# In-projection as a Strassen product over pairs of token blocks with HGRN beside it, and RWKV as two streams beside the output projection

## The chip, the cores and the metric

The kernel runs on one core of one Trainium2 chip. A time is the device time of one execution in microseconds (us); the kernel before took 2655.96 us, the median of three runs (2654.36 to 2656.32). The engines are TensorE (PE: matmuls, with its weight loads shown apart as PEld), VectorE (DVE), ScalarE (ACT), GpSimd (POOL) and SyncE (SP). In this kernel POOL and SP mostly issue DMAs. Each engine works through its own list of instructions in order; the order of the lists is fixed when the program is built.

## The reference

One decoder layer over 2048 tokens of width 1024, all in float32.

```python
h = RMSNorm(x)
proj = h @ w_in                                  # 1024 x 3840
q, f, i, g | r, k, v, wd, ad, gd = split(proj)   # 4 x 512 HGRN | 3 x 512 + 64 + 64 + 128 RWKV
o_hg = HGRN2(q, f, i, g)       # 4 heads of 128, gated linear recurrence over tokens, chunkwise
rw = rw + (token_shift(rw) - rw) * mu
o_rw = RWKV7(r, k, v, wd, ad, gd)   # 8 heads of 64, S = S diag(w) + (S a) b^T + v k^T, y = S r
x = x + concat(o_hg, o_rw) @ w_out
x = x + ConvFFN(RMSNorm(x))    # up 1024 -> 2 x 2816, causal conv of 3, silu gate, down 2816 -> 1024
out = RMSNorm(x)
```

Both recurrences carry a state from token to token, so the blocks of 512 tokens must be taken in order.

## The kernel before, in words

The tokens are four blocks of 512 (`BLK`). A float32 product is made of three matmuls of a reduced float32 type: each operand is split into a high and a low part (`split`, lines 250 to 256: a cast on ACT, a subtraction on DVE), and `mm3` (lines 268 to 272) multiplies high by high, high by low and low by high.

The first stage is `phase1`. Its generator `dense` works through a list of jobs: for each block, 30 columns of 128 of the in-projection ("P" jobs, 8 steps of `mm3` over the width of 1024 each, accumulated in a PSUM bank `pj`), the transposes of the next block's normalized input, and, two blocks behind, the output projection of a block (`out_block`) and the norm of its result. The weights of the in-projection are split in the first block and stored in DRAM (`Win`); the later blocks load the two parts again.

Beside it run two more generators. `hg_unit` handles one HGRN head of one block, 16 units in all. `rw_super` handles four RWKV heads of one block, 8 of them in all, one after the other. A `rw_super` scales and groups its inputs, forms the chunk matrices `M`, sends their diagonal 32 x 32 pieces through DRAM into another layout (`Ed`, then `E`), inverts them by 31 dependent steps of two small DVE operations each (lines 800 and 802, tiles `etmp` and `Ti`), transposes the result (`TZ`, `TTs`), runs four groups of small matmuls with evictions between them, and then the eight steps along the tokens (lines 903 to 910, tile `XH`), each needing the one before; a group norm and a gate end it (`yo`).

The main loop of `phase1` takes one step of `rw_super`, one of `hg_unit`, and then fills PE with dense matmuls worth `TICK` = 2000 ns. A step is what lies between two `yield`s. A scheduler then settles each engine's order, roughly in this order, by when it thinks that inputs are there. So the dense matmuls stand between all the small ones until the end of the stage.

Behind `phase1` come the output projection of the last block (`wacc`, line 1268), the up projection of the FFN as a Strassen product over pairs of blocks (seven products of half size in place of eight, tiles `ua`, `ub`, `ud`), and the down projection, also Strassen (`da`, `db`). This part is the same in both kernels.

Of the kernel before, what the change touches and what calls it, by code (L numbers as in the profile page):

```python
# [10 lines left out]
U32 = mybir.dt.uint32  # L11
# [56 lines left out]
def tile_layer(ctx, tc, consts, x, norm1_w, w_in, hg_lb_logits, hg_norm_w, rw_shift_mu, rw_w0, rw_w2,  # L68
               rw_a0, rw_a2, rw_g2, rw_k_k, rw_k_a, rw_r_k, rw_ln_w, rw_ln_b, w_out, norm2_w, w_up,
               conv_w, conv_b, w_down, final_norm_w, out, pairs=(0, 1, 2, 3), heads=(0, 1, 2, 3),  # L70
               stages=("1", "2"), dbg=None):
# [9 lines left out]
    xp_ = cx.enter_context(tc.tile_pool(name="xp", bufs=1, reuse_waits="tile"))  # L81

    def row_tile():
        return xp_.tile([P, 4, D], F32, tag="xt", name="xt", bufs=1)

    ident = cp.tile([P, P], F32, name="ident")
    cst = cp.tile([P, C_ID], F32, name="cst")
    dma(ident, consts[:, C_ID:C_ID + P])
    first = row_tile()
    for i in range(4):  # L90
        dma(first[:, i, :], x[0, i * P:(i + 1) * P, :])
    cen = cst[:, C_CEN:C_CEN + P]
    blk1 = cst[:, C_ONE:C_ONE + P]
    s1m = cst[:, C_S1:C_S1 + P]
    dgm = cst[:, C_DG:C_DG + 64]
    dg32 = cst[:, C_D32:C_D32 + 32]
    scanm = cst[:, C_SCAN:C_SCAN + 512]
# [42 lines left out]
    with tc.tile_pool(name="vp", bufs=1, reuse_waits="tile") as vp, tc.tile_pool(name="ps0", bufs=1, space=PSUM, reuse_waits="tile") as pools["ps"]:  # L140
# [12 lines left out]
        for i in range(4):  # L153
            V.tensor_scalar_mul(first[:, i, :], first[:, i, :], rstd(vp, first[:, i, :], "nst", sqb=2))
# [6 lines left out]

    lnx = cp.tile([P, 4], F32, name="lnx")
    for r0 in (0, 64):
        S.copy(lnx[r0:r0 + 64, :], vt[64 - r0:128 - r0, off["lnw"] + 1:off["lnw"] + 8:2])
# [109 lines left out]
    def phase1(c1):  # L274
        hp = c1.enter_context(tc.tile_pool(name="hp", bufs=1, reuse_waits="tile"))
        wp = c1.enter_context(tc.tile_pool(name="wp", bufs=2, reuse_waits="tile"))
        sp = c1.enter_context(tc.tile_pool(name="sp", bufs=1, reuse_waits="tile"))
        rp = c1.enter_context(tc.tile_pool(name="rp", bufs=1, reuse_waits="tile"))
        ps = c1.enter_context(tc.tile_pool(name="ps1", bufs=1, space=PSUM, reuse_waits="tile"))

        w2a2 = hp.tile([P, 512], F32, name="w2a2")
        g2 = hp.tile([P, 512], F32, name="g2")
        lastc = hp.tile([P, 64], F32, name="lastc")
# [7 lines left out]
        for t_ in (TTs, Af):  # L291
            nc.gpsimd.memset(t_, 0.0)
# [13 lines left out]
        def stg(tag, name, bufs):  # L306
            return sp.tile([P, BLK], F32, tag=tag, name=name, bufs=bufs)
# [1315 lines left out]
```

## Time and profile before

| | us |
|---|---|
| median of three runs | 2655.96 |
| the profiled execution, its own time | 2662.58 |
| span of the profiled execution | 2660.8 |
| PE busy in the span | 2560.2 (96%) |
| DVE busy | 1952.9 (73%) |
| ACT busy | 1389.2 (52%) |
| POOL busy | 380.4 (14%) |

Busy time is the union of the instructions' durations on an engine. PE records overlap (the next matmul starts before the one before has ended), so a PE that is shown busy all the time need not be at its peak, and the distance between two starts says more than a duration. Idle time of an engine is put down to the instruction that ended it. The first `wacc` matmul starts at 1325.8 us, which ends `phase1`; the first `ua` matmul starts at 1373.8 us, and the last down-projection step of the up stage ends at about 2275 us.

### The profile page before, as it was taken

To read this page: it belongs to the slowest core of one execution; us is meant where nothing else is said; L and a number is where in the kernel's file an instruction comes from. 1 tells how busy PE (TensorE), PEld (TensorE's weight loads), DVE (VectorE), ACT (ScalarE), POOL (GpSimd) and SP (SyncE) were. 2 spreads that over 40 slices of the span, in tenths; PEclk is the share of its full clock that TensorE was granted. 3 is DMA by queue.
4 is the path that set the end of the run, shared out by engine and by line. 5 is a ranking of instruction groups with operands and counts; after the bars stand their busy time and mean duration, and the time that the engine had idled before them with its cause. 6 is when DMAs were issued, how large, how long until landed. Compare 5 with 4: busy or idle time off the path is not lost. (4 is left out here: it accounts for less than half of the span.)

```text
span 2660.8 us, 51050 instructions
## 1 busy us (share of the span) xinstructions
PE 2560.2 (96%) x19595; PEld 2061.2 (77%) x19595; DVE 1952.9 (73%) x3728; ACT 1389.2 (52%) x2274; POOL 380.4 (14%) x686
## 2 busy tenths in 40 slices
PE   7999999989999999999899999999999999999998
PEld 5777777766777777777678888887888887888887
DVE  4877667576567765767678789987998887766556
ACT  5566453545535555445456754456545544545444
POOL 6433222212222122222100000000000000000000
PEclk9999999999999999999999999999999999999999
DMA  8645443445643456744493468646763553998665
GB/s 303 204 165 170 158 143 120 130 148 203 199 143 126 156 196 199 276 131 136 154 309 113 143 204 266 233 154 225 245 203 131 166 189 127 327 320 286 197 191 186
DMA packets 312714, 510.59 MB, mean 192 GB/s; under 512 B 46879, under 2 KB 143509, under 8 KB 312469
## 3 DMA queue, kind: packets, MB, share of 16 engines
q1 hardware_dynamic: 257937, 328.99, 37.4%
q0 software_dynamic: 54464, 178.32, 20.4%
q8 instruction: 154, 2.52, 0.4%
q14 instruction: 91, 0.75, 0.1%
q10 hardware_dynamic: 68, 0.02, 0.0%
HBM read 372.99 MB, written 134.22 MB: 191 GB/s over the span
## 5 line engine op out<-in xcount | busy, mean ns | idle before, releaser
L270 PE MATMUL pj<-hh,wh 128*128 128x512 f32 x960 | 393.4, 410 | 6.2 <-ACT rkv L122 3.3
L271 PE MATMUL pj<-hl,wh 128*128 128x512 f32 x960 | 377.8, 394 | 1.3 <-issue 1.3
L272 PE MATMUL pj<-hh,wl 128*128 128x512 f32 x960 | 377.5, 393 | 0.0
L270 PE MATMUL ua<-Bh,uwh 128*128 128x512 f32 x704 | 276.4, 393 | 4.4 <-ACT m L122 3.1
L272 PE MATMUL ua<-Bh,uwl 128*128 128x512 f32 x704 | 274.6, 390 | 0.0
L271 PE MATMUL ua<-Bl,uwh 128*128 128x512 f32 x704 | 274.3, 390 | 0.0
L270 PEld LDWEIGHTS pj<-hh,wh 128*128 128x128 f32 x960 | 181.5, 189 | 55.2 <-issue 8.7
L272 PEld LDWEIGHTS pj<-hh,wl 128*128 128x128 f32 x960 | 181.1, 189 | 40.6 <-issue 1.7
L271 PEld LDWEIGHTS pj<-hl,wh 128*128 128x128 f32 x960 | 181.6, 189 | 34.3 <-DVE hl L488 0.5
L254 ACT CAST uwh<-uraw 128x512 fp32r<-128x512 f32 x220 | 134.2, 617 | 128.9 <-PE ua L271 55.7
L255 DVE TENSOR_TENSOR dal<-draw,dah 128x512 fp32r<-128x512 f32 x138 | 95.4, 691 | 113.4 <-ACT dah L254 113.2
L255 DVE TENSOR_TENSOR uwl<-uraw,uwh 128x512 fp32r<-128x512 f32 x220 | 147.6, 688 | 34.9 <-ACT uwh L254 34.8
L254 ACT CAST dah<-draw 128x512 fp32r<-128x512 f32 x138 | 85.7, 621 | 164.9 <-PE da L271 80.6
L270 PEld LDWEIGHTS ua<-Bh,uwh 128*128 128x128 f32 x704 | 132.2, 188 | 34.1 <-ACT m L122 5.7
L272 PEld LDWEIGHTS ua<-Bh,uwl 128*128 128x128 f32 x704 | 132.3, 188 | 28.1 <-DVE uwl L255 0.4
L271 PEld LDWEIGHTS ua<-Bl,uwh 128*128 128x128 f32 x704 | 132.3, 188 | 26.7
L270 PE MATMUL ud<-Bh,uwh 128*128 128x512 f32 x352 | 138.1, 392 | 0.0
L272 PE MATMUL ud<-Bh,uwl 128*128 128x512 f32 x352 | 137.2, 390 | 0.0
L271 PE MATMUL ud<-Bl,uwh 128*128 128x512 f32 x352 | 137.1, 390 | 0.0
L1493 POOL DMA_DIRECT2D gd<-y x2 | 1.1, 540 | 946.8 <-DVE y L1491 946.8
L271 PE MATMUL da<-dbl,dah 128*128 128x512 f32 x332 | 129.5, 390 | 0.2 <-DVE dbl L255 0.2
L272 PE MATMUL da<-dbh,dal 128*128 128x512 f32 x332 | 129.3, 389 | 0.0
(584 smaller groups left out, 6233.9 us busy)
## 6 DMA issues: line engine op xcount, KB each, us to landing
uraw<-in_w_up_dram SPq DMA_DIRECT2D x176, 256.0 KB, 3.1
woraw<-in_w_out_dram POOLq DMA_DIRECT2D x96, 256.0 KB, 3.6
br<-gd SPq DMA_DIRECT2D x88, 256.0 KB, 4.2
draw<-Sg SPq DMA_DIRECT2D x88, 256.0 KB, 3.3
draw<-Tw SPq DMA_DIRECT2D x88, 256.0 KB, 4.0
gd<-y SPq DMA_DIRECT2D x86, 256.0 KB, 2.9
Sg<-br SPq DMA_DIRECT2D x72, 256.0 KB, 2.1
xt<-x1d SPq DMA_DIRECT2D x32, 512.0 KB, 6.7
```

The costliest lines, as they stand in the source:

```text
L254: S.copy(hi, src)
L255: V.tensor_sub(lo, src, hi.bitcast(F32))
L270: TE.matmul(acc, lh, rh, start=first, stop=False, skip_group_check=skip)
L271: TE.matmul(acc, lh, rl, start=False, stop=False, skip_group_check=skip)
L272: TE.matmul(acc, ll, rh, start=False, stop=last, skip_group_check=skip)
L1493: (dma if end is None else nc.gpsimd.dma_start)(gd_[2 * h + b][fb * P:(fb + 1) * P, :], ys[0][:, b * BLK:(b + 1) * BLK])
```

## The change

`phase1` is replaced by two stages, `phase_a` and `phase_b`. What follows them is unchanged.

**`phase_a`** makes the in-projection of two blocks (1024 tokens) at a time as a Strassen product: two columns of 128 and two blocks of 512 form a 2 x 2 product over two halves of the width, with seven products (`a11`, `a12`, `s2`, `s1`, `s3`, `a22`, `s4`) of 4 steps of `mm3` each. There are 15 pairs of columns (`ORDER`) and two passes, 30 x 7 x 4 x 3 = 2520 matmuls of 128 x 512 in place of 30 x 4 x 8 x 3 = 2880. The seven combinations of the input (`Ah`, `Al`) stand in SBUF; in the first pass they are made by `begin`, in the second from DRAM (`rebuild`). In the first pass the weights and their sums are split and stored (`Win`), in the second loaded. The norm of the later two blocks and the split of `w_out` (`Wout`) run aside. Results are finished per column pair (`column_done`) and stored in DRAM. HGRN's 16 units run beside it, and read their inputs back from DRAM; a unit may start when its `g` column is stored. `hk`, `hf`, `hq`, `hv` and `hg` have one buffer each.

**`phase_b`** then runs RWKV as two streams, each with its own buffers: stream 0 has heads 0 to 3, stream 1 heads 4 to 7; stream 1 starts 24 steps (`LEAD`) later, and a lock lets one stream at a time through the eight steps along the tokens. Beside them run the output projection of blocks 0, 1 and 2, with weights loaded as stored parts, and the norms of blocks 0 and 1.

```diff
+    TICKS = (3200.0, 2200.0)
...
+                    for k in range(KD):
+                        tp = bank("mm")
+                        for i in range(4):
+                            TE.transpose(tp[:, i * P:(i + 1) * P], rows_x[4 * b + i][:, k * P:(k + 1) * P], ident)
+                        act(hT[k][b], tp, AF.Copy, scale=vec("n1", k))
+                        if b == 0:
+                            split_to(Bh[k // 4][:, k % 4, :], Bl[k // 4][:, k % 4, :], hT[k][0])
...
+                    def prod(acc, nm, bi, first, n=n, ops=ops):
+                        wh, wl = ops.pop(nm)
+                        for k in range(4):
+                            mm3(acc, (wh[:, k, :], wl[:, k, :]), (Bh[bi][:, k, :], Bl[bi][:, k, :]),
+                                first and k == 0, k == 3, True)
+                            if k < 3:
+                                yield 680
...
+        credit, at = 0.0, 28
+        while any(alive.values()):
+            if alive["h"]:
+                try:
+                    next(hg_)
+                except StopIteration:
+                    alive["h"] = False
+            credit += TICKS[at >= 15 * 28]
+            while alive["d"] and credit > 0:
+                try:
+                    credit -= next(dn_)
+                    at += 1
+                except StopIteration:
+                    alive["d"] = False
+
+    TICK_B = 1200.0
...
+            while lock:
+                yield None
+            lock.append(s_)
...
+        LEAD = 24
+        gens = [stream(0), stream(1)]
+        dn_ = dense()
+        alive, n, credit = [True, True, True], 0, 0.0
+        while any(alive):
+            for s_ in range(2):
+                if alive[s_] and (s_ == 0 or n >= LEAD):
+                    try:
+                        next(gens[s_])
+                    except StopIteration:
+                        alive[s_] = False
+            credit += TICK_B
...
-        def fill(ns):
-            nonlocal credit
-            credit += ns
-            while alive["d"] and credit > 0:
...
-        while any(alive.values()):
-            for key, g in (("r", rw_), ("h", hg_)):
-                if alive[key]:
-                    try:
-                        next(g)
-                    except StopIteration:
-                        alive[key] = False
-            fill(TICK)
```

Three places in the engines' orders matter below. The first is PE's list at the very start. Before, `hg` and `rw` are PSUM banks lent to the transposes of the first block, and `pj` is the in-projection:

```order
L156 MATMUL vps<-ident,rows 128x128
L264 MATMUL hg<-ident,xt 128x128 x2
L264 MATMUL rw<-ident,xt 128x128
L264 MATMUL hg<-ident,xt 128x128 x2
L264 MATMUL rw<-ident,xt 128x128 x3
L264 MATMUL hg<-ident,xt 128x128 x2
L264 MATMUL rw<-ident,xt 128x128 x2
L264 MATMUL hg<-ident,xt 128x128 x2
L264 MATMUL rw<-ident,xt 128x128 x2
L270 MATMUL pj<-hh,wh 128x512 x2
L271 MATMUL pj<-hl,wh 128x512
```

Now, with `mm` the banks of stage A, and `Al_75` to `Ah_78` the tiles that hold the rows of blocks 0 and 1 at first:

```order
L361 MATMUL mm<-ident,Al_77 128x128 x12
L361 MATMUL mm<-ident,Ah_78 128x128 x12
L361 MATMUL mm<-ident,Al_77 128x128 x2
L361 MATMUL mm<-ident,Ah_78 128x128 x2
L361 MATMUL mm<-ident,Al_77 128x128 x2
L361 MATMUL mm<-ident,Ah_78 128x128 x2
L264 MATMUL mm<-Ah_63,uwh 128x512
L265 MATMUL mm<-Al_64,uwh 128x512
L266 MATMUL mm<-Ah_63,uwl 128x512
```

Before, the first dense matmul followed half of one block's transposes; now all 64 transposes of two blocks (the first 32 stand ahead of these rows) come first.

The second place is PE's list at the end of HGRN. Before, the last unit's matmuls (`hg`) stand among dense ones (`pj`) and RWKV's (`rw`):

```order
L272 MATMUL pj<-wh,hl 128x512
L1081 MATMUL rw<-part,group 128x512
L1082 MATMUL rw<-part,group 128x512
L1081 MATMUL rw<-part,group 128x512
L1082 MATMUL rw<-part,group 128x512
L1081 MATMUL hg<-part,ones 128x512
L1082 MATMUL hg<-part,ones 128x512
L270 MATMUL pj<-wh,hh 128x512
L271 MATMUL pj<-wl,hh 128x512
L272 MATMUL pj<-wh,hl 128x512
```

Now a whole unit, from its first transposes (L656) to its norm (L269, L270), and with it the unit ahead of it, stands alone between the last dense matmul of stage A and the first matmul of RWKV (L891, which follows the last L270):

```order
L269 MATMUL hg<-part,ones 128x512
L270 MATMUL hg<-part,ones 128x512
L656 MATMUL hg<-ident,hv 128x128 x4
L695 MATMUL hg<-hq,hk 32x32 x16
L695 MATMUL hg<-hX 32x16 x80
L702 MATMUL hg<-hX 32x32 x8
L749 MATMUL hg<-ident,hk 128x128 x4
L751 MATMUL hg<-hX 64x64 x4
L760 MATMUL hg<-VT,KT 128x128 x4
L770 MATMUL hg<-Af,VT 128x128
L771 MATMUL hg<-hq,SH 128x128
```

After the last dense matmul PE's list has the norm of unit 13 and all of units 14 and 15 (16 units are counted from 0), and then RWKV.

The third place is DVE's list around an inversion. Before, the 62 small operations (`etmp`, `Ti`) have HGRN's between them (`hf`, `hk`, `hq`, `hX`):

```order
L802 TENSOR_TENSOR Ti<-Ti,etmp 128x10x11
L972 TENSOR_TENSOR hf<-hf 128x4x64
L800 TENSOR_TENSOR etmp<-E,Ti 128x108
L1035 TENSOR_TENSOR hk<-hk,Sf 128x512
L802 TENSOR_TENSOR Ti<-Ti,etmp 128x9x12
L1036 TENSOR_TENSOR hq<-hq,hf 128x512
L800 TENSOR_TENSOR etmp<-E,Ti 128x96
L963 TENSOR_TENSOR hX<-hq,hf 128x256
L802 TENSOR_TENSOR Ti<-Ti,etmp 128x8x12
```

Now, where stream 1's first inversion ends (`TTs_9617` is stream 1's) and stream 0's second begins:

```order
L1019 TENSOR_TENSOR Ti<-Ti,etmp 128x16
L1023 STREAM_TRANSPOSE TZ<-Ti 128x512
L1029 STREAM_TRANSPOSE TTs_9617<-TZ 32x16x32 x4
L1008 MEMSET Ti 128x512
L1098 COPY XH<-Xc 128x2x64
L1010 COPY Ti<-cst 128x16 x2
L951 TENSOR_TENSOR M<-rw,cst 128x2x2x128 x4
L1089 TENSOR_TENSOR M<-rw,cst 128x2x4x64
L1092 TENSOR_TENSOR AR<-rw,AR 128x2x4x64
L1017 TENSOR_TENSOR etmp<-E,Ti 128x31
L1019 TENSOR_TENSOR Ti<-Ti,etmp 128x31
```

L1089 and L1092 are stream 1's, and read PE's result of the matmuls that use its new `TTs`; stream 0's inversion (the last two rows) stands behind them. HGRN's operations are gone from this stage.

1164 lines of the change are left out of this document (625 added, 539 removed).

## The prediction

> **What bounds the kernel now.** I read the busy times by stage first, then the distance between the starts of neighbouring instructions, then the groups by line, then single waits. Busy time by stage (columns: stretch, its length, PE, PEld, DVE, ACT and POOL busy with their counts, granted PE clock, DMA share, GB/s):
>
> ```profile
> 0.00:20.00 20.00, 4.55 (x17) 3.04 (x17) 8.13 (x27) 11.99 (x28) 12.78 (x27) 1.00 0.91 305
> 20.00:1326.00 1306.00, 1239.79 (x13778) 976.18 (x13778) 888.12 (x2106) 668.67 (x1105) 351.85 (x631) 0.99 0.52 171
> 1326.00:1374.00 48.00, 45.49 (x196) 35.95 (x196) 34.03 (x57) 23.85 (x42) 1.82 (x3) 1.00 0.92 308
> 1374.00:2275.00 901.00, 892.79 (x3946) 734.46 (x3945) 780.75 (x1177) 500.59 (x762) 0.19 (x1) 1.00 0.57 188
> 2275.00:2661.00 386.00, 377.54 (x1663) 311.57 (x1662) 241.83 (x364) 184.09 (x340) 13.80 (x26) 0.99 0.75 252
> ```
>
> The change replaces the first 1326 us and leaves the other 1335 as they are. The first stage is bound by PE: 95% busy, DVE 68%, ACT 51%. What PE does there, as the same view gives it for the instructions on one bank name (dense `pj`, RWKV `rw`, HGRN `hg`, in this order):
>
> ```profile
> 20.00:1326.00 1306.00, 900.45 (x3616) 654.74 (x3616) 88.03 (x167) 100.13 (x160) 0.99 0.52 171
> 20.00:1326.00 1306.00, 271.35 (x6153) 211.69 (x6152) 121.40 (x196) 159.53 (x244) 0.99 0.52 171
> 20.00:1326.00 1306.00, 136.81 (x4008) 115.28 (x4008) 60.59 (x180) 54.92 (x116) 0.99 0.52 171
> ```
>
> A dense matmul with a few transposes costs 900.45/3616 = 0.249 us beside the small work; in the FFN, which has none, 892.79/3946 = 0.226 us. RWKV costs 271/8 = 34 us of PE a super, HGRN 137/16 = 8.6 us a unit. DVE's share is held by many lines; first and last of RWKV's 31 groups and of HGRN's 16:
>
> ```profile
> L802 DVE TENSOR_TENSOR Ti<-Ti,etmp 128x126 f32<-128x126 f32 (+22 forms) x248 | 63.3, 255 | 4.5
> L685 DVE MEMSET W<- 128x16 f32 x8 | 0.6, 72 | 11.9 <-PE rw L893 11.9
> L972 DVE TENSOR_TENSOR hf<-hf 128x256 f32<-128x256 f32 x112 | 47.3, 422 | 1.2
> L1057 DVE COPY Sc<-SH 128x128 f32<-128x128 f32 x16 | 3.5, 218 | 0.2
> ```
>
> Their sums are 429 us (53.6 a super) and 296 us (18.5 a unit). Durations on DVE overlap a little, as starts in the timeline show (start, duration):
>
> ```profile
> 1219.84 0.24 DVE L802 TENSOR_TENSOR Ti<-Ti,etmp 128x81 f32<-128x81 f32 x1
> 1220.12 0.24 DVE L800 TENSOR_TENSOR etmp<-E,Ti 128x78 f32<-128x78 f32 x1
> ...
> 1254.36 0.67 DVE L255 TENSOR_TENSOR wl<-woraw,wh 128x512 fp32r<-128x512 f32 x1
> 1254.96 0.67 DVE L413 TENSOR_TENSOR xh<-pj,xh 128x512 f32<-128x512 f32 x1
> ```
>
> An independent 128x512 operation takes 0.60 us, 0.87 of its duration of 0.69 (the groups' mean, below); the dependent steps of the inversion take 0.28 each, however idle the engine is.
>
> **Stage A, dense part.** Durations that the next parts use (a subtraction of a split; an eviction and a cast on ACT; four transposes, the next group starting 0.56 us later):
>
> ```profile
> L255 DVE TENSOR_TENSOR wl<-woraw,wh 128x512 fp32r<-128x512 f32 x96 | 65.8, 688 | 32.9 <-ACT wh L254 32.5
> L122 ACT ACTIVATE h<-pj,vt 128x512 f32<-128x512 f32 x16 | 10.3, 684 | 8.2 <-PE pj L264 7.8 <-ACT h L122 0.4
> L254 ACT CAST wh<-wraw 128x512 fp32r<-128x512 f32 x60 | 36.9, 619 | 75.4 <-PE pj L271 36.5 <-DMA wraw<-in_w_in_dram 15.2 <-issue 9.6
> 127.42 0.63 PE L1042 MATMUL hg<-ident,hk 128*128 128x128 f32 x4 [1.59 <-DVE hk L1035]
> 127.98 0.68 PE L1044 MATMUL hg<-hX 128*64 128x64 f32 x8
> ```
>
> The Strassen form removes 2880 - 2520 = 360 matmuls, 82 to 90 us at the two rates. RWKV's stalls are gone from beside it, HGRN's stay, so I take 0.236, between them. DVE stays below PE: in the first pass a pair needs some 22 us of it (seven splits and seven sums at 0.69, 2.6 for finishing columns, 2.6 aside, 0.4 unit of HGRN), or 19 by starts, against 84 x 0.236 + 0.4 x 8.6 + 1 = 24 us of PE. The stores and loads of weights leave POOL's queue for SP's, where a store that waits for a split holds the loads behind it; two operands of lag cover that, and without the cover each product (12 matmuls, 2.8 us) would wait for a landing of some 3 us.
>
> The start is later. Before, PE's first matmul waits for a small load, and in the first 20 us it has 4.55 us of work:
>
> ```profile
> L156 PE MATMUL vps<-ident,rows 128*128 128x128 f32 x1 | 0.4, 448 | 10.7 <-DMA rows<-in_hg_lb_logits_dram 10.7
> ```
>
> Now 64 transposes and 16 evictions on ACT (0.69 each, with eight casts of 0.62 and eight half squares of about 0.6, together 21 us) stand ahead of the first product, so it starts near 40. The first pair needs 16 subtractions and 20 splits more on DVE, 36 x 0.60 = 22 us; at 65 us PE has done 96 matmuls. Bounds: 42 us (96 x 0.226 behind a start at 20) and 85 (nothing beside anything). The rest is 2424 x 0.236 = 572, fourteen units of HGRN 14 x 8.6 = 120, and 128 transposes at 0.14 are 18. The last dense matmul is at 65 + 572 + 120 + 18 = **775 us**.
>
> [...]
>
> **Stage A, HGRN alone.** As the order shows, units 14 and 15 run with no dense matmul beside them. Nothing in the trace shows a unit alone. From below it costs PE's 8.6 us; from above the 54 us that unit 15 took beside dense work, from its first DVE operation at 1257.4 to its last matmul at 1311.1. Its own chain: about 14.5 us of dependent DVE work by starts (of 18.5), some 4 us of ACT (evictions and casts of 0.60, Ln and Exp), 5 us of PE, and the wait for its predecessor's store, since `hk` and `osq` share a buffer:
>
> ```profile
> L945 DVE TENSOR_SCALAR hk<-hf 128x512 f32<-128x512 f32 x16 | 6.8, 423 | 4.1 <-DMA oT<-osq 4.0
> oT<-osq POOLq DMA_DIRECT2D x4, 256.0 KB, 3.0
> 1257.42 0.47 DVE L945 TENSOR_SCALAR hk<-hf 128x512 f32<-128x512 f32 x1 [0.59 <-DMA oT<-osq]
> L1063 PE MATMUL hg<-hq,SH x128: 270/275/580, 134.0 to 1311.1; 128*128 128x128 f32 x128
> ```
>
> That is 27 us; two, and the end of unit 13, make **60 us** (17 to 112). PE idles for most of it; before, dense matmuls filled these gaps.
>
> **Stage B.** PE's work is 271 + 576 x 0.226 + 14 = 415 us, DVE's 429 + 52 (splits of the heads' outputs, residual sums, norms) = 481, or 418 by starts. Eight supers with no overlap set the other bound. One super's chain alone: front (sigmoids, scan, some fourteen 1.0 to 1.2 us operations) 26, `M` 6.5, the trip through DRAM 6.4, inversion 62 x 0.28 = 17.4, transposes 3.9, four groups of matmuls with evictions between them 16.5, eight steps at 0.87 (see below) 7, group norm 14: 97 us, so 776 for eight. The rows for the trip, two of the evictions, a front operation, `M`, a transpose, and two steps:
>
> ```profile
> Ed<-M SPq DMA_DIRECT2D x32, 64.0 KB, 3.3
> E<-Ed SPq DMA_DIRECT2D x16, 256.0 KB, 3.1
> L122 ACT ACTIVATE UV<-rw 64x512 f32<-64x512 f32 x32 | 19.0, 593 | 0.6 <-PE rw L845 0.2
> L122 ACT ACTIVATE ZT<-rw 32x256 f32<-32x256 f32 x32 | 12.0, 375 | 6.0 <-PE rw L819 5.5
> L717 DVE TENSOR_TENSOR ai<-ai 128x1024 f32<-128x1024 f32 x8 | 9.8, 1220 | 0.0
> L733 DVE TENSOR_TENSOR M<-rw,cst 128x512 f32<-128x512 f32 x64 | 40.4, 685 | 11.0 <-PE rw L730 10.9
> L812 DVE STREAM_TRANSPOSE TTs<-TZ 32x512 f32<-32x512 f32 x32 | 22.5, 703 | 0.8
> 1286.17 0.29 DVE L910 TENSOR_TENSOR XH<-rw,WC 128x128 f32<-128x128 f32 x1
> 1287.04 0.29 DVE L910 TENSOR_TENSOR XH<-rw,WC 128x128 f32<-128x128 f32 x1
> ```
>
> DVE's order says how the two streams mesh. It repeats three parts. X: stream 1's front (14 us by starts), two sums and eight steps of stream 0, stream 1's `M`, and the trip through DRAM, before which stream 1 can't invert: 36 us. Y: stream 0's group norm (14), its front and its `M`, and between them stream 1's inversion, of which 8.5 us are left over, and transposes: 49 us. Z: stream 1's groups of matmuls, for whose first result (L1089) DVE waits some 12 us with stream 0's inversion queued behind it, then that inversion with stream 1's steps in it, 21, and transposes: 37 us. A round is 122 us. Stage B is stream 0's first front to transposes (56, its first squares being done ahead), three rounds (366), a last X (36), the last inversion alone (21), groups, steps and norm (42), and 49 dense matmuls that PE's list has behind them (11): **532 us**. It lies nearer to 418 than to 776 because the two fronts and inversions do overlap in the list. The output projection is hidden in it, and of no use to it: it can't fill DVE's waits.
>
> **The sum.** 775 + 60 + 532 + 1335 = 2702 us of span. The profiled run took 2662.58 for a span of 2660.8, so 2704 for this one; it lay 6.6 above the median, so **2697**, 41 us slower than before.
>
> **Rivals.** *The streams fill each other's gaps* (faster). If DVE never waits in the order above, stage B needs its 418, plus stream 0's head start and stream 1's end at half use, some 50: 468. With stage A ending at 763 (at 0.231) and a tail of 50, the span is 2616 and the time **2611**. For it: DVE reaches 781/901 = 87% in the FFN. Against it: there the order runs ahead of need, here 62-step chains, a trip of 6.4 us and the L1089 wait stand in one queue. It turns to faster when a round is below 110 us.
>
> *One queue, two streams* (slower still). If waits of both streams add up in DVE's and PE's lists, since an output-projection matmul placed early waits for heads just stored, a round grows by 25 us to 147; three and a half rounds give 88 more: **2785**. For it, waits of one engine for another's list are long now (24 here, the longest 12.4 us):
>
> ```profile
> ACT rkv L122 <- PE pj L272: 135.6, 24, 12.4
> ```
>
> Against it, the lists were sorted by readiness.
>
> *PE runs cold.* After a PE idle stretch the profile grants half the clock:
>
> ```profile
> 1285.00:1290.00 5.00, 2.77 (x61) 2.01 (x56) 4.49 (x14) 2.78 (x7) 0.54 (x1) 1.00 0.93 305
> 1290.00:1295.00 5.00, 3.85 (x9) 3.08 (x10) 2.17 (x5) 2.97 (x5) 0.00 (x0) 0.51 0.80 273
> ```
>
> Here 2.2 us idle were followed by a clock of 0.51. Such gaps are rare now, 0.99 on the mean; units 14 and 15 and stream 0's head start are made of them, and stage B has 415 us of PE work in 532. If half of stage B runs at half clock, the some 20 us of PE on a super's chain cost 10 more, 10 x 5 (four supers and the head start) plus 10 in the tail: **2757**. [...]
>
> *The change does not do what it says*: HGRN beside the product for fourteen units of sixteen is settled by the list, so this has no time of its own.
>
> **How the numbers follow.** Forecast 0.50 (own range 2660 to 2735, 0.05 of it within 0.2% of before, about what a measurement can tell from no change), streams filling gaps 0.28, one queue 0.12, cold PE 0.10. Faster 0.28, same 0.05, slower 0.67. The range takes in the faster case with its bounds for the start and the tail, and most of the slower ones: 2605 to 2790.
>
> **What would show it.** The last dense matmul of stage A near 775 us; a stretch of some 60 us with only `hg` matmuls; RWKV's last matmul near 1350; DVE about 87 to 90% busy in stage B with waits of about 10 us at L1089 and at the first `etmp` after `E`; a granted clock near 1 in the first 750 us and lower after. A stage B below 490 us, or a stage A that ends before 750, makes the prediction wrong.

## The result, and the profile after

The changed kernel takes 2879.03 us (median of four runs, 2873.91 to 2889.03) against 2656.14 for the kernel before (median of four runs): a ratio of 1.084, 95% interval 1.080 to 1.088, 223 us slower. The sign is the one forecast; the time is far outside the range. Its profiled execution has a span of 2872.1 us, 170 more than the 2702 of the sum.

Busy time by stage of the changed kernel (columns as before: stretch, its length, PE, PEld, DVE, ACT and POOL busy with their counts, granted PE clock, DMA share, GB/s):

```profile
20.00:798.00 778.00, 727.59 (x6089) 578.10 (x6090) 516.42 (x1144) 390.82 (x742) 85.05 (x157) 0.97 0.81 277
798.00:862.00 64.00, 29.77 (x531) 24.06 (x531) 40.47 (x110) 21.12 (x43) 8.56 (x15) 0.63 0.23 75
862.00:1543.00 681.00, 501.98 (x6785) 363.13 (x6784) 448.40 (x1001) 325.20 (x496) 104.44 (x195) 0.85 0.49 161
1543.00:1590.00 47.00, 45.33 (x195) 35.86 (x195) 33.05 (x55) 24.13 (x43) 0.00 (x0) 1.00 0.92 302
1590.00:2491.00 901.00, 895.82 (x3965) 736.22 (x3964) 784.57 (x1183) 504.57 (x767) 1.08 (x2) 1.00 0.58 189
2491.00:2872.00 381.00, 373.49 (x1646) 308.25 (x1644) 237.18 (x358) 180.96 (x334) 12.92 (x24) 1.00 0.75 254
```

The last dense matmul of stage A starts at 798.2 us, HGRN alone lasts until 861.7, the RWKV stage until the first `wacc` matmul at 1542.8, and the rest takes 1329.4. Of the 170 us, stage A has 23, the HGRN tail 3.5, the RWKV stage 149 (681.0 where 532 were forecast), and the rest takes 5.6 less. In the RWKV stage no engine is near full: PE 74%, DVE 66%, ACT 48%, at a clock of 0.85. The same view for the instructions on one bank name (`pj`, `rw`, `xp`, `yp`, in this order) tells what PE did there:

```profile
862.00:1543.00 681.00, 196.92 (x640) 117.85 (x640) 16.45 (x24) 14.21 (x32) 0.85 0.49 161
862.00:1543.00 681.00, 240.52 (x4096) 171.92 (x4094) 90.83 (x120) 149.23 (x232) 0.85 0.49 161
862.00:1543.00 681.00, 56.59 (x1024) 41.41 (x1024) 18.43 (x64) 0.85 0.49 161
862.00:1543.00 681.00, 55.85 (x1024) 44.33 (x1024) 9.54 (x16) 0.85 0.49 161
```

RWKV is the sum of the last three rows, 353 us for eight supers, where the kernel before had 271; a projection matmul or transpose takes 196.92/640 = 0.31 us. Both are larger in a stage with a clock of 0.85. The groups by line of that stage show where engines stood still (behind the bar: busy, mean ns of one; then the idle time ahead of them and what ended it):

```profile
L264 PE MATMUL pj<-wh,oh 128*128 128x512 f32 x192 | 88.1, 471 | 46.9 <-ACT oh L248 17.3 <-DMA wh<-Wo03h 9.3 <-DVE xh L1182 5.7
L249 DVE TENSOR_TENSOR ol<-oraw,oh 128x256 fp32r<-128x256 f32 x48 | 19.9, 421 | 14.5 <-ACT oh L248 14.4
L248 ACT CAST oh<-oraw 128x256 fp32r<-128x256 f32 x48 | 18.6, 402 | 68.7 <-DMA oraw<-oT 54.0 <-PE pj L265 14.6
L1132 DVE TENSOR_TENSOR XH<-xp,WC 128x128 f32<-128x128 f32 x64 | 18.4, 288 | 29.8 <-PE xp L1125 29.1
L1182 DVE TENSOR_TENSOR xh<-pj,xh 128x512 f32<-128x512 f32 x24 | 16.4, 689 | 23.7 <-PE pj L266 23.6
L1089 DVE TENSOR_TENSOR M<-rw,cst 128x512 f32<-128x512 f32 x16 | 11.0, 688 | 34.3 <-PE rw L1086 34.3
```

Four of the six lines belong to the projection (`pj`, `oh`, `ol`, `xh`): PE, ACT and DVE each wait for it, with the streams' instructions queued behind. The round can be read off the timeline of DVE, from one scan of stream 1's front to the next:

```profile
924.81 1.22 DVE L898 TENSOR_TENSOR_SCAN mk<-cst,ai 128x512 f32<-128x512 f32 x1 [0.73 <-ACT ai L120]
...
1063.94 1.23 DVE L898 TENSOR_TENSOR_SCAN mk<-cst,ai 128x512 f32<-128x512 f32 x1 [1.71 <-ACT ai L120]
...
1217.48 1.22 DVE L898 TENSOR_TENSOR_SCAN mk<-cst,ai 128x512 f32<-128x512 f32 x1
...
1380.87 1.22 DVE L898 TENSOR_TENSOR_SCAN mk<-cst,ai 128x512 f32<-128x512 f32 x1 [2.13 <-ACT ai L120]
```

Rounds of 139, 154 and 163 us, where 122 were forecast. The first ends before the projection really begins: 36 of its 576 matmuls have run by then.

### The profile page after: what moved, and what is told of

It is laid out like the page before. It is cut to its first block, busy times and chain, and to the rows that moved or that the text cites. A ratio compares the mean times of both kernels' runs of the same rounds, so it can differ in the third digit from the quotient of the medians.

```text
span 2872.1 us, 51606 instructions
## 1 busy us (share of the span) xinstructions
PE 2580.7 (90%) x19235; PEld 2051.2 (71%) x19235; DVE 2066.9 (72%) x3869; ACT 1460.2 (51%) x2451; POOL 216.1 (8%) x405
## 4 chain that ended last, share of the span: by engine, by line
PE 39%; DMA 6%; DVE 4%; issue 1%; ACT 1%; SPq 1%; POOL 0%; DVEq 0%; ACTq 0%; POOLq 0%
PE ua L264 4%; PE ua L266 4%; PE ua L265 4%; PE da L264 3%; PE da L265 3%; PE da L266 3%; PE ud L265 2%; PE ud L266 2%; PE ud L264 2%; PE db L264 2%; PE db L265 2%; PE db L266 2%; DMA br<-gd 1%; PE ub L265 1%; PE ub L266 1%
## 5 line engine op out<-in xcount | busy, mean ns | idle before, releaser
L264 PE MATMUL mm<-Ah,uwh 128*128 128x512 f32 x840 | 349.6, 416 | 29.4 <-ACT m L120 20.0
L266 PE MATMUL mm<-Ah,uwl 128*128 128x512 f32 x840 | 337.6, 403 | 6.6 <-DMA uwl<-Win54l 4.4
L265 PE MATMUL mm<-Al,uwh 128*128 128x512 f32 x840 | 336.7, 401 | 0.6 <-DVE Al L242 0.6
L248 ACT CAST uwh<-uraw 128x512 fp32r<-128x512 f32 x295 | 180.7, 618 | 195.5 <-PE ua L265 58.7
L249 DVE TENSOR_TENSOR uwl<-uraw,uwh 128x512 fp32r<-128x512 f32 x295 | 198.4, 686 | 53.4 <-ACT uwh L248 52.6
L264 PEld LDWEIGHTS mm<-Ah,uwh 128*128 128x128 f32 x840 | 160.9, 192 | 72.4 <-ACT m L120 25.3
L266 PEld LDWEIGHTS mm<-Ah,uwl 128*128 128x128 f32 x840 | 160.9, 192 | 48.7 <-DMA uwl<-Win54l 4.5
L265 PEld LDWEIGHTS mm<-Al,uwh 128*128 128x128 f32 x840 | 161.2, 192 | 34.9 <-DVE Al L242 1.7
L248 ACT CAST uwh<-s 128x512 fp32r<-128x512 f32 x118 | 72.4, 620 | 133.1 <-PE ua L265 62.6
L264 PE MATMUL pj<-wh,oh 128*128 128x512 f32 x192 | 88.1, 471 | 46.9 <-ACT oh L248 17.3
```

Source lines behind the costliest of these rows:

```text
L248: S.copy(hi, src)
L249: V.tensor_sub(lo, src, hi.bitcast(F32))
L264: TE.matmul(acc, lh, rh, start=first, stop=False, skip_group_check=skip)
L265: TE.matmul(acc, lh, rl, start=False, stop=False, skip_group_check=skip)
L266: TE.matmul(acc, ll, rh, start=False, stop=last, skip_group_check=skip)
```

## The experiments

Except for ticks_low each kernel was timed once, so the lengths of stages are compared. The RWKV stage goes from its first matmul to the first `wacc` matmul. The same code does not repeat exactly: the RWKV stage of the changed kernel took 681.0, 686.8 and 691.6 us in three runs that leave it alone, and the last dense matmul of an untouched stage A came between 793 and 806. Differences under 10 us are not read. The 681.0 from which differences are taken below is the lowest of its three, so a gain against it may be up to 10 us larger, and a loss as much smaller.

| run | last dense matmul | RWKV stage | its last RWKV matmul, from its first | time |
|---|---|---|---|---|
| changed kernel | 798.2 | 681.0 | 658.5 | 2879.03 |
| no_proj | 798.5 | 577.6 | 571.1 | 2772.58 |
| fill | 801.7 | 582.4 | 575.6 | 2779.28 |
| one_stream | 804.2 | 370.7 | 362.5 | 2570.75 |
| one_fill | 799.7 | 364.3 | 356.1 | 2561.89 |
| proj_only | 797.1 | 626.7 | 618.5 | 2824.27 |
| proj_loose | 800.2 | 665.3 | 649.8 | 2860.75 |
| no_proj_late | 794.9 | 583.3 | 576.6 | 2772.09 |
| late_rhs | 800.9 | 682.4 | 647.4 | 2877.42 |
| pool_side | 799.4 | 704.0 | 681.7 | 2902.47 |
| prefetch | 803.7 | 703.0 | 612.8 | 2903.17 |
| tick_b_high | 800.3 | 700.3 | 693.5 | 2896.29 |
| dve_fill | 793.0 | 586.2 | 579.4 | 2783.18 |
| act_fill | 802.7 | 582.4 | 575.6 | 2784.69 |
| all_fill | 799.9 | 588.1 | 581.4 | 2796.77 |
| dve_placed | 805.6 | 604.6 | 594.7 | 2803.06 |
| all_placed | 798.2 | 610.1 | 600.0 | 2803.21 |
| no_hgrn | 681.0 | 686.8 | 663.4 | 2703.84 |
| ticks_low | 864.7 | 691.6 | 668.2 | 2888.16 |

**The streams alone.**

```diff
-        alive, n, credit = [True, True, True], 0, 0.0
+        alive, n, credit = [True, True, False], 0, 0.0
```

> The output projection, the norm and the sums of token blocks 0 to 2 are left out of the RWKV stage (their outputs are set to zero by 56 stores), the two streams stay as they are. In the changed kernel this stage took 681 us, from the first RWKV matmul to the first matmul of the next stage, with 179 us of PE idle and a granted clock of 0.85. Theory 1 (PE runs cold: idle stretches halve its clock, and what PE does on the streams' chains takes longer): there are more idle stretches now, the clock falls below 0.8, and the stage stays near 600. Theory 2 (the projection's matmuls and loads stand in the streams' queues): the stage falls to the 520 that I had forecast, three rounds of about 122. Theory 3 (the round of two streams was sized too small in itself): the stage stays above 630 and a round near 150.

577.6 us: between the theories, 103 less than the changed kernel, and yet 46 more than the 532 forecast for the whole stage. So the two streams were sized too small, and the projection is far from hidden. The row of the stage, and stream 1's scan, its next scan and what stood between the end of stream 0's steps and stream 1's inversion:

```profile
862.00:1440.00 578.00, 347.64 (x6145) 262.62 (x6146) 398.91 (x904) 283.54 (x385) 1.26 (x2) 0.75 0.14 42
```

```profile
1195.23 1.22 DVE L898 TENSOR_TENSOR_SCAN mk<-cst,ai 128x512 f32<-128x512 f32 x1 [1.64 <-ACT ai L120]
...
1228.95 0.23 DVE L1135 COPY Xc<-XH 128x128 f32<-128x128 f32 x1
1235.95 1.23 DVE L242 TENSOR_TENSOR part<-yo,part 128x1024 fp32r<-128x1024 f32 x1 [6.77 <-ACT part L241]
1241.61 1.23 DVE L1145 TENSOR_TENSOR yo<-yo 128x1024 f32<-128x1024 f32 x1 [4.44 <-ACT yo L120]
1242.76 0.18 DVE L1017 TENSOR_TENSOR etmp<-E,Ti 128x31 f32<-128x31 f32 x1
...
1333.61 1.22 DVE L898 TENSOR_TENSOR_SCAN mk<-cst,ai 128x512 f32<-128x512 f32 x1 [1.74 <-ACT ai L120]
```

A round is 138 us here. Part X, from stream 1's scan to its inversion, is 1242.8 - 1195.2 = 47.5 us where 36 were forecast: after stream 0's last step DVE works 2.5 of 13.6 us, since stream 0's norm stands in its list ahead of stream 1's inversion and waits twice for ACT. The trip through DRAM was also longer than forecast: its first store is issued at 1226.3 us and the last packet of its loads ends at 1235.4, 9.1 us for 6.4 (the forecast had one store and one load behind each other; there are four stores and two loads). So of the 11.5 us some 3 are the trip's, and the 7.4 from 1235.4 to 1242.8 are the norm's. Parts Y and Z take 91 together, against 86.

**Free matmuls beside the streams.** Matmuls of zeros, written at the projection's places of the program:

```diff
+            acc = bank("pj")
+            for q in range(24):
+                TE.matmul(acc, group, zt, start=q == 0, stop=q == 23)
+                if q % 3 == 2:
+                    yield 680
```

> As no_proj, but the 576 projection matmuls are replaced by as many matmuls of the same size, into the same two banks and at the same places of the program, whose operands are always there (no loads, splits or evictions). Theory 1: the clock rises to over 0.9 and the stage is shorter than in no_proj, by some 40 us, though PE does 130 us more. Theory 2: if it is the waiting of the projection for its data that hurts, the stage is as in no_proj within 15 us; if it is its mere time on PE, it is as in the changed kernel, near 680. Theory 3: as in no_proj.

```profile
865.00:1448.00 583.00, 471.86 (x6794) 359.64 (x6794) 399.07 (x904) 284.43 (x385) 1.25 (x2) 0.89 0.14 41
```

The program has 648 of them, not 576, and they did not stay at the projection's places: waiting for nothing, they were put between 870 and 1261 us, 375 of them ahead of the time from which the projection runs (1064 us). PE is busy 124 us more, the clock goes from 0.75 to 0.89, and the stage stays where it was. The same holds within one round: stream 1's round from 1064 to 1204 us, full of such matmuls at a clock of 0.95, took 140 us, and that of no_proj from 1060 to 1195 us 136 at 0.79. Neither the matmuls' time on PE nor the half clock bounds the streams, or the two cancel; the next pair tells.

**One stream, bare and with matmuls.**

```diff
-        alive, n, credit = [True, True, True], 0, 0.0
+        alive, n, credit = [True, False, False], 0, 0.0
```

> As no_proj with the second stream left out as well (two of the four heads' pairs are not computed): four supers one behind the other, and nothing beside them. My prediction put one super's chain alone at 97 us: 4 x 97 = 390 from its first matmul to its last. Theory 1: the clock is near 0.6, and a super takes 110 to 115 us, 450 in all. Theory 2 leaves it at 390. Theory 3: the chain itself was sized too small, over 120 us a super at a clock that is not the reason.

> one_stream with 576 matmuls of zeros, free of dependencies, in the gaps of the one stream; some 65 of them fall behind its end. One stream alone took 362.5 us from its first matmul to its last at a clock of 0.68, 92 a super. Theory 1 (the half clock lengthens a chain): the clock rises over 0.9 and a super takes 82 to 85 us. If a super stays at 91 to 93, the half clock costs the chain nothing that matters, or the filler takes back what it gives.

```profile
865.00:1229.00 364.00, 182.19 (x3073) 138.12 (x3073) 204.23 (x450) 138.52 (x188) 4.26 (x8) 0.69 0.13 40
```

```profile
862.00:1220.00 358.00, 294.48 (x3649) 226.50 (x3649) 204.05 (x451) 138.96 (x188) 4.26 (x8) 0.90 0.13 40
```

A super takes 362.5/4 = 91 us at a clock of 0.69 and 356.1/4 = 89 at 0.90: the chain was sized well (97). The matmuls of one_fill all run by 1093 us, none behind the stream's end; so the first two supers are the cleaner pair, 183 us at 0.69 (869 to 1053 us in one_stream) and 180 at 1.00 (866 to 1046 in one_fill). The lower clock costs some 2 us a super, less than the runs repeat, net of what the free matmuls take on PE. Theory 1 falls. One super uses DVE for 204/4 = 51 us; two streams in a round of 138 use it for 100.

**What order can mend.** The block that makes `RHS` and `UV` is written later, so that ACT comes to stream 0's norm first:

```diff
+            def late_rhs():
                 RHS = tile_("KB", [8, 2, P], "RHS")
...
             for j in range(31):
...
+                if j == 7:
+                    RHS, UV = late_rhs()
```

> no_proj (streams alone, 577.6 us for the stage, a round of 137) with the block that makes RHS, UV and the first correction (lines 976 to 1005) written behind the eighth step of its stream's inversion instead of ahead of it. In the trace of no_proj DVE stood still 29.6 us ahead of the norm's split and 25.2 us ahead of the norm's product, since on ACT the evictions of the other stream's RHS and UV stood ahead of the norm's square and cast, and the other stream's inversion stood behind the norm on DVE. If that order is what made the round 14 us longer than the 122 forecast, those two idle sums fall under 20 us together, the round to about 126 and the stage to 535 to 545. Rival: the round is bound elsewhere and the idle moves to other rows; the stage stays above 565.

> The same edit on the whole changed kernel (stage 681 us). By the order of ACT 35 to 45 us less, 640; by the rival 670 or more.

The idle of 55 us ahead of the norm's two operations (no_proj) fell to 28, and came back elsewhere, ahead of the next front's scan and of the norm's sum with `BV`. The groups in no_proj, then those in no_proj_late (whose lines behind the inversion are numbered two higher):

```profile
L898 DVE TENSOR_TENSOR_SCAN mk<-cst,ai 128x512 f32<-128x512 f32 x16 | 19.5, 1220 | 9.5 <-ACT ai L120 9.5
L242 DVE TENSOR_TENSOR part<-yo,part 128x1024 fp32r<-128x1024 f32 x8 | 9.8, 1223 | 29.6 <-ACT part L241 29.6
L1152 DVE TENSOR_TENSOR yo<-yo,BV 128x1024 f32<-128x1024 f32 x8 | 9.7, 1213 | 3.3 <-ACT yo L120 3.3
L1145 DVE TENSOR_TENSOR yo<-yo 128x1024 f32<-128x1024 f32 x8 | 9.7, 1219 | 25.2 <-ACT yo L120 25.2
```

```profile
L898 DVE TENSOR_TENSOR_SCAN mk<-cst,ai 128x512 f32<-128x512 f32 x16 | 19.5, 1221 | 30.2 <-ACT ai L120 30.2
L1147 DVE TENSOR_TENSOR yo<-yo 128x1024 f32<-128x1024 f32 x8 | 9.8, 1225 | 16.8 <-ACT yo L120 16.8
L1154 DVE TENSOR_TENSOR yo<-yo,BV 128x1024 f32<-128x1024 f32 x8 | 9.8, 1225 | 18.8 <-ACT yo L120 18.8
L242 DVE TENSOR_TENSOR part<-yo,part 128x1024 fp32r<-128x1024 f32 x8 | 9.8, 1223 | 11.0 <-ACT part L241 11.0
```

The stage stayed at 583, and at 682 with the projection. The order of ACT makes this wait and not the length of the round: with half of the wait gone, as much idle stands elsewhere in the same round. What sets the round, as I read it, is that a chain of 91 us runs through lists which also hold the other chain's 50 us of DVE work, and finds its own waits filled only in small part: 91 + 50 = 141, near the 136 to 138 measured. That sum fits, but no run proves it.

**The projection taken apart.** First without norm and sums, then with matmuls that do not read what was loaded:

```diff
-                if nb < 2:
-                    yield from norm_block(nb)
...
-                            mm3(accs[q], [t_[:, q * P:(q + 1) * P] for t_ in held[k]], wts, k == 0, k == KD - 1)
+                            mm3(accs[q], (group, group), (zt, zt), k == 0, k == KD - 1)
```

> The norm and the sums of the finished blocks are left out of the RWKV stage, the output projection with its loads stays. no_proj showed 578 us for the stage without all three, the changed kernel 681. Theory 2a (the projection itself holds the streams back: its matmuls stand in PE's list and wait for their loads and splits): the stage stays above 655. Theory 2b (the norm and the sums do, with their DVE and ACT work and their chains of loads and stores on SP's queue): the stage falls to 600 to 620.

> Everything stays beside the streams (loads, splits, evictions, norm, sums), but the projection's 576 matmuls read a fixed tile of zeros in place of the operands just loaded, so that PE never waits for them; ten buffers of splits become eight to make room. Theory 2a: if PE's waiting for the projection's data holds the streams back, the stage falls to under 610. Rival (the extra work on DVE and ACT, 50 and 42 us more busy time, and the loads): it stays above 645.

Each half carries about half of the cost: 49 us for the projection alone, 54 more for norm and sums. Without PE's waits for data the stage is 16 us shorter, of the 103. The run is not quite the changed kernel without these waits: it has eight buffers for ten, and 192 of its matmuls, free to go, ran before 1000 us (28 in the changed kernel). Theory 2a, that PE's waits do most of it, falls.

**Moving the side work, or asking earlier.**

```diff
-                            held.append(split(wp, raw, [P, 256], "o", 10))
+                            S.copy(hi, raw)
+                            nc.gpsimd.tensor_sub(lo, raw, hi.bitcast(F32))
```

> The changed kernel with the DVE work of the projection's side moved to POOL, which is idle in this stage: the subtractions of its splits (48 of 128x256), the scaling of the norm (8 of 128x1024) and the four sums (16 of 128x512), some 39 us of DVE. no_proj is 103 us shorter than the changed kernel, proj_only 54, and proj_loose only 16, so it is not PE that waits. Theory Q (side work stands in DVE's list between the two streams' steps, with its waits): the stage falls by 35 to 60 us, to 620 to 645. Rival (ACT's share and the loads hold the streams): it falls by less than 15.

```diff
+                            while len(raws_) < min(k + 3, KD):
...
+                                dma(raw, oT[nb][k_ * P:(k_ + 1) * P, i2 * 256:i2 * 256 + 256])
...
+                    yield 1500
                     for q in range(2):
                         V.tensor_add(xh[q], accs[q], xh[q])
```

> The changed kernel with the projection's operands asked for earlier: each load of a row block of heads is written two blocks ahead of its split, and 1500 units of time lie between a group's last matmul and its eviction on DVE. In the changed kernel ACT stood still 68.7 us ahead of the casts of these blocks (mostly for their loads) and DVE 23.7 us ahead of the evictions and 14.5 us ahead of the splits. If these waits in the lists of ACT and DVE are what costs, the stage falls to 640 to 650 and the idle ahead of the casts under 30; if it is the mere work, it stays within 10 us of 681.

```diff
-    TICK_B = 1200.0
+    TICK_B = 2400.0
```

> The changed kernel with twice the pace at which the projection is put between the streams' steps (2400 units a step for 1200). Its last matmul now comes 21 us behind the streams' last. If the pace only shifts the cost, the streams end later by what the projection ends earlier, and the stage stays within 10 us of 681; if the projection was merely late, the stage falls to 660.

All three made the stage longer, by 19 to 23 us. With POOL, 37 us of work left DVE's list (19.9 + 5.8 + 11.1), whose busy time fell by only 12 (448 to 436), in part since operations that stayed became slower (shown in the last section), and on POOL the moved ones took longer themselves (a subtraction 894 ns for 421). POOL also issues the loads of the projection's weights, and the moved subtractions now stand between these; PE's idle ahead of its first matmuls for such a load hardly grew (9.3 to 10.2 us). How much of the 23 us each makes was not separated. With prefetch the streams ended 46 us sooner (612.8), with 424 of the stage's 448 us of DVE work done by then, and the projection 89 us behind them: the delay of the streams went and came back as the projection's own end. ACT stood still even longer ahead of the casts. At the double pace the projection was done 40 us ahead of the streams, which took 35 us more: DVE waited 62.9 us for a step's product, for 29.8 before. The group of the casts in prefetch, then that of the steps at the double pace:

```profile
L248 ACT CAST oh<-oraw 128x256 fp32r<-128x256 f32 x48 | 18.4, 402 | 103.4 <-DMA oraw<-oT 91.1 <-PE pj L265 9.4 <-issue 2.9
```

```profile
L1132 DVE TENSOR_TENSOR XH<-xp,WC 128x128 f32<-128x128 f32 x64 | 18.5, 289 | 62.9 <-PE xp L1125 62.4
```

So the pace shifts the cost between the streams and the projection, and saves none of it.

**Work without data.** Additions on DVE and copies on ACT that wait for nothing:

```diff
+                    V.tensor_add(fz[:, 0], fz[:, 1], fz[:, 1])
+                    act(fz[:, 2], fz[:, 3], AF.Copy)
```

> no_proj (streams alone, 577.6 us) with 72 additions of 128x512 on DVE that depend on nothing, spread as the projection is: 50 us of busy time, 43 by starts, as much as the projection, the norm and the sums put on DVE. If DVE's list is the path (it shows 69% busy, but the streams' chains stand in it), the stage grows by 35 to 50, to 613 to 628. If the cost is in waits for data, it grows by less than 15.

> The same with 72 copies of 128x512 on ACT, some 45 us, as much as the projection's casts, squares and evictions. If ACT's list (49% busy) is on the path too, the stage grows by 20 or more; if only DVE's is, by less than 10.

> 72 additions on DVE, 72 copies on ACT and 576 matmuls beside the streams, none of which waits for anything: all of the projection's work without its data. The changed kernel with the data is at 681. If the work is what costs, the stage is at 640 or more; if the data, under 600.

These three grew by 5 to 11 us, but say little: having nothing to wait for, the operations were placed early. The 72 on DVE ran between 805 and 905 us, 42 of them in the idle HGRN tail. The additions and copies were repeated, each held behind the stream's operation that precedes it:

```diff
+                    tc.add_manual_dep(i_.ins, mark["d"].ins.name, NOSYNC, reason="place")
```

> no_proj (577.6 us) with 72 additions of 128x512 on DVE, 43 us by starts, each held in DVE's list at its place among the streams' operations of rounds 2 to 4, with no data to wait for. If DVE's list is the path and mere work counts, the stage is at 610 to 625. If DVE has room for it between the streams (31% idle), it is under 590.

> As dve_placed, and 72 copies on ACT held at their places in the same way, and 576 matmuls that wait for nothing. If work is what costs, the stage is at 640 or more, near the 681 of the changed kernel; if the waits for data are, under 610; between the two, the part above 578 is the work's and the rest the waits'.

```profile
862.00:1472.00 610.00, 470.27 (x6721) 356.20 (x6720) 441.63 (x978) 324.71 (x456) 1.98 (x3) 0.85 0.14 42
```

27 us for DVE's work alone (43 by starts), and 32 with ACT's and PE's added. PE, DVE and ACT are now as busy as in the changed kernel but for 32, 7 and 0 us (first stage view), and the stage is 71 us shorter. So of the projection's 103 us a third is the price of DVE's and ACT's work in lists that have room on paper. The matmuls were not held: 383 of the 576 ran before 1064 us, so their price at the projection's own places is not in the 32.

The other 71 are a remainder, and that they come with the data (waits for loads and for each other) is argued and not shown. The trace says where they stand: against all_placed DVE works 7 us more and is idle 64 us more. Of its idle in the changed kernel 38 us stand right ahead of the projection's splits and evictions (14.5 and 23.7, the rows above) and 8 ahead of the norm and the sums. Some 12 are the longer end (the next stage starts 22.5 us behind the streams' last matmul, 10.1 in all_placed). The projection's traffic did not slow the streams' own trip through DRAM: to 1440 us a store of `Ed` lands in 2.0 us (2.2 in no_proj), a load of `E` in 3.6 (4.0). Which waits make the 71 was not taken apart beyond proj_loose and prefetch.

**Stage A, without HGRN and with HGRN placed denser.**

```diff
-            for n in range(16):
+            for n in range(0):
                 while len(units) <= n:
```

> The 16 units of HGRN are left out of the first stage (their rows of the output are set to zero), the dense product stays. My sum had 0.236 us for a dense matmul beside HGRN and 8.6 us of PE for a unit: by it the last dense matmul comes at 65 + 572 + 18 = 655 us. The changed kernel's trace has 93 us of PE time between dense matmuls that HGRN takes in this stretch and 40 us of idle: if HGRN costs what it shows, the last dense matmul is at 798 - 93 = 705; if the dense product's own stalls are the 40 us, the idle stays near 40; if HGRN's waits make them, it falls under 15 and the end is near 675.

```diff
-    TICKS = (3200.0, 2200.0)
+    TICKS = (2200.0, 1500.0)
```

> The first stage asks for a step of HGRN every 2200 and 1500 units of dense work instead of every 3200 and 2200, so that all 16 units stand beside dense matmuls. If the stretch at the end of the stage (63 us in which only two units run) is what it seems, the last dense matmul moves from 798 to about 813 us, the RWKV stage starts by 818 instead of 862, and the whole kernel is about 45 us faster than the changed one. Rival: the same steps beside dense work make dense matmuls wait, and less than 20 us are won.

Without HGRN the last dense matmul is at 681.0, so fourteen units beside it cost 117 us, 8.4 each. The stage from matmul 96 on without HGRN, and the group of the first matmul of each triple:

```profile
64.00:681.00 617.00, 587.76 (x2490) 465.37 (x2489) 268.49 (x453) 243.74 (x439) 45.98 (x85) 0.98 0.90 312
```

```profile
L264 PE MATMUL mm<-Ah,uwh 128*128 128x512 f32 x808 | 327.5, 405 | 28.2 <-ACT uwh L248 10.2 <-ACT m L120 8.8 <-DMA uwh<-Win02h 3.6
```

PE works 587.76/2490 = 0.236 us a matmul, and stands still 29 us more: products wait for their cast operand (10.2 us), and for the accumulator's copy `m` (8.8 us), which must be read before the next product adds to it. With ticks_low all sixteen units do stand beside dense matmuls, and the last of these comes at 864.7: 184 us for sixteen units, 11.5 each. PE's waits there (what waited and for what; total, times, longest):

```profile
PE hg L656 <- DMA hv<-HG0v: 23.8, 4, 8.4
PE hg L656 <- DMA hv<-HG1v: 17.9, 3, 7.1
```

A unit placed too early waits on PE for its `hv` to be loaded, 42 us in all, and the dense product stands behind it. The rival was right: at this pace nothing of the 63 us of tail is won (181 us for sixteen units with it, 184 without). A placement without the waits for `hv` was not tried. This kernel measures 2888.16 us (median of four runs), a ratio to the kernel before of 1.088 (1.086 to 1.090).

No version with the whole computation came near the kernel before. The parts tell why: stage A with HGRN ends at 861.7 and the bare streams take 571, which is 1433 before any output projection, and the kernel before had done all of it by 1326.

## Why the prediction was wrong

- **The start** was right: matmul 96 of the product starts at 64.2 us, forecast 65.
- **Stage A's dense part** was 23 us short. Its sum has no term for the product's own stalls, 29 us in no_hgrn. PE's time came out right, 588 us for 572 + 18 = 590, but with some luck: only 64 of the 128 transposes come behind matmul 96, the others ahead of the first product. They took 12.2 us, which leaves 0.237 us a matmul. HGRN at 8.6 a unit was right (8.4). With the 0.249 us a matmul of the kernel before, the same sum gives 807, and with the FFN's 0.226 it gives 751; the first is nearer to 798, though not for its reason: it has no stalls. Weight loads take 465/617 = 75% of the stage without HGRN, and the other quarter was not free for HGRN: fourteen units still cost 8.4 us each.
- **The HGRN tail** was right (63.5 for 60). The one try to fill it with dense work won nothing.
- **One super's chain** was right within 6%: 91 us for 97.
- **The round of two streams**, 122 us, failed first. Part X was forecast at 36 us, ended by the trip through DRAM; it takes 47.5 without any projection, some 3 of them since the trip itself is longer and 7 since the norm of stream 0 stands ahead of the inversion and waits for ACT. no_proj_late took half of such waits away and the stage did not get shorter, so this order alone is not to blame. In all 46 of the 149 us: 577.6 measured without any projection against 532 forecast with it.
- **"The output projection is hidden in it, and of no use to it"** was the step that failed most, 103 us. Its matmuls alone can be hidden (fill: 5 us, not measurable, at places that were earlier). Its casts, subtractions, evictions, norms and sums are not: 32 us as mere work, and by subtraction 71 with its data. By place, 43 of the 103 us lie in the two rounds (154 and 163 against 136 and 138 in no_proj), 40 between stream 1's last scan and the streams' last matmul (139 against 99), 16 behind that, and 4 ahead of the rounds. I counted DVE's 52 us in the bound by busy time (418 by starts), but not in the round.
- **The rest** was right: 1329.4 for 1335.

Of the rivals, *one queue, two streams* comes nearest to the mechanism, and 25 us a round was its price: measured, 18 and 25. It put the wait on PE's matmuls, which are worth 16 us (proj_loose), where ACT's casts and DVE's evictions wait longer; and it came short in time (2785) because the bare round was too small as well. *The streams fill each other's gaps* is refuted by no_proj: the bare streams take 578 where it had 468 for all. *PE runs cold* was right that the clock falls (0.63 in the tail, 0.85 in the stage, 0.69 for one stream) and had the price wrong: some 2 us a super, for the 10 that were forecast.

Of the signs named, the waits at L1089 came (9.97 us at 1181.1, 34.3 in all), the wait for `E` at the first `etmp` came once (12.4 us), and so did the falling clock; RWKV's last matmul came at 1520 us for 1350, and DVE was not 87 to 90% busy but 66%. That is the sign which should have been doubted beforehand: it took for granted that in-order lists can be filled. Both signs that were to make the prediction wrong (a stage B below 490 us, a stage A ahead of 750) lie on the faster side; none was named for a slower stage.

## What to carry to other kernels

In this case a chain of dependent steps cost little more than its own work while it ran beside work that is long, dense and ready: before, PE was busy 1239.8 of 1306 us (95%) with RWKV's chains among 3456 projection matmuls; now there are 576, and they depend on the chains. Where two chains share in-order lists, a first estimate from this case is the chain alone plus the other's work on the shared engine (91 + 50 for a round of 138), and for side work added to such a list well over half of its time (27 of 43 us, on a DVE that was idle for 31% of no_proj's stage). Price an engine's work by its place in the list: here free matmuls beside a chain were free (one_fill 364.3 us for one_stream's 370.7), and ready additions on a DVE that was a third idle were not (dve_placed 604.6 for no_proj's 577.6).

## What the hardware showed

In pool_side some operations of DVE that ran at the same time as elementwise work on POOL took longer (12 `Ti` steps 915 ns, the others 253). Groups by line in the changed kernel, then with POOL's subtractions, scalings and sums (pool_side):

```profile
L1019 DVE TENSOR_TENSOR Ti<-Ti,etmp 128x126 f32<-128x126 f32 (+22 forms) x248 | 63.1, 255 | 6.1
L922 DVE SCALAR_TENSOR_TENSOR BV<-mk,vt,AR 128x512 f32<-128x512 f32 x16 | 11.7, 748 | 0.1
```

```profile
L1019 DVE TENSOR_TENSOR Ti<-Ti,etmp 128x126 f32<-128x126 f32 (+22 forms) x248 | 70.8, 285 | 6.9
L951 DVE TENSOR_TENSOR M<-rw,cst 128x512 f32<-128x512 f32 x64 | 40.9, 684 | 25.0 <-PE rw L948 24.7
L1171 POOL TENSOR_TENSOR ol<-oraw,oh 128x256 fp32r<-128x256 f32 x48 | 42.3, 894 | 212.7 <-ACT oh L1170 212.4
L922 DVE SCALAR_TENSOR_TENSOR BV<-mk,vt,AR 128x512 f32<-128x512 f32 x16 | 13.7, 871 | 0.1
```

The mean step of the inversion went from 255 to 285 ns, L922 from 748 to 871, while L951, which reads PSUM, stayed at 684 (683 before). The growth is that of a few: 12 of the 248 `Ti` steps overlap one of POOL's operations and take 915 ns on the mean (the longest 4.69 us), the other 236 take 253; of L922, 5 overlap and take 1143 ns, the others 748. Not every overlap costs: L936 reads two SBUF tiles too, and the two of its operations that overlap stayed at 1216 ns. The same subtraction takes 894 ns on POOL and 421 on DVE. The PSUM reader was untouched: 10 of L951's operations overlap, at 684 ns.

The half clock of PE hardly lengthened a chain: the first two supers of one stream take 91.6 us each at a clock of 0.69 and 89.8 at 1.00. In the stretch with HGRN alone the clock stands at half or full: 0.50 from 803.3 to 830.6 us, 1.00 to 837.4, 0.50 to 857.9. PE had not stood still ahead of the first fall: in the 5.1 us from 798.2 to 803.3 it worked 3.35 us. What the half clock costs a chain that leaves PE idle half of its time (one_stream: busy 182 of 364 us) is some 2 us a super here, and filling PE with matmuls to keep the clock up bought nothing (fill 582.4 us at a clock of 0.89, no_proj 577.6 at 0.75).
